# Bias tables fetched a head pair earlier, reciprocals read back in longer pieces, and a planner with dearer transfers through HBM

## The chip, the cores and the metric

The kernel runs on one core of a Trainium2 chip. The core has five engines that work side by side, each through its own list of instructions in order: TensorE (PE in the profile: matrix products into the accumulation banks of PSUM), VectorE (DVE), ScalarE (ACT), GpSimd (POOL) and SyncE (SP). In this kernel SP does nothing but issue transfers (DMA); POOL and, seldom, ACT issue some too. All transfers share the core's 16 DMA engines. An instruction waits until what it reads has been written and until the buffer it writes is free; whatever stands behind it on the same engine waits with it.

The metric is the time of one execution in microseconds (us). Before the change it was measured in three runs, and the median is 567.25 us.

## What is computed

One layer of a hybrid decoder on 512 positions of width 1024, all in fp32: a normalisation, one combined projection, three groups of heads that work in parallel, an output projection, and a feed-forward part.

```python
h = rmsnorm(x, norm1_w)
aq, ak, av, bq, bk, bv, br, ba, cq, ck, cv = split(h @ w_in)
y_a = dilated_attention(aq, ak, av, bias_a)      # 6 heads
y_b = gla(bq, bk, bv, br, ba, ...)               # 4 heads, gated linear attention
y_c = moba_attention(cq, ck, cv, bias_c)         # 6 heads
x = x + concat(y_a, y_b, y_c) @ w_out
x = x + square(relu(rmsnorm(x, norm2_w) @ w_ff1)) @ w_ff2
return rmsnorm(x, final_norm_w)
```

What matters here are the 12 softmax heads of groups A and C. For each head the kernel computes scores q·k, adds a bias that depends only on the distance between query and key (mask and head group are folded into it), takes exp and the row sums, multiplies by v, and divides by the row sums.

## The kernel before, in words

*Precision.* A matrix product of fp32 values is made of three products: each operand is split into a rounded high part and a remainder (`xh`, `xl`, `wh`, `wl`), and high × high, low × high and high × low are added up. So every 512 KB piece of weights is loaded by SP into a `wraw` tile, rounded by ScalarE (`wh`) and subtracted by VectorE (`wl`). This is `parts` (line 310), called by `cut` (332) in a fixed order of pieces.

*Stages.* First the projection for the gated linear attention (up to some 30 us), then the value projection of the first heads, then for each of the six head pairs p = 0 to 5 the query and key projections (`qk_proj`, 1151), the second value projection, the output projection and the feed-forward part, each followed or interleaved by what depends on it. The softmax heads run from some 84 to 206 us, between and beside the projections.

*Attention of a pair.* `attention(e)` (886) runs as two streams, e = 0 and 1, one for each head of a pair. For each pair it takes a buffer `nb` of 128 × 512, and SP loads into it the head's bias table from `tab` in HBM (each partition reads the same row of distances shifted by one, 2 KB). It then waits for the pair's queries and keys, and for four blocks of 128 queries computes scores into one of two score banks (`sps`, tag "s"); `softmax` (983) on VectorE adds the bias from `nb`, takes the minimum and frees the bank, and ScalarE takes exp and the row sum.

*Turning.* The products with the values need the probabilities transposed. For pairs 0 to 3 (`XP`) VectorE transposes blocks of 32 × 32 (`moved`, 1009) into the tiles `tb` and `t2s`, and `through` (1026) puts the blocks in place by way of HBM: SP writes the tile to a scratch `turn`, and POOL reads it back in four transfers into `thb` or `th2` (shown as `th`). Pairs 4 and 5 are transposed on TensorE (`ptp`). `values` (938) multiplies by v for two pairs at a time (`po`).

*Reciprocals.* `row_sums` (990) takes the reciprocals of the row sums, transposes them, and SP writes them to a scratch `zt` in HBM in four transfers of 1 KB. Two reads (`rzb<-zt`) then spread each head's 512 values over 64 partitions. `mix_out` (649) multiplies the value products by them.

*Who sets the order.* The order of instructions on every engine is made when the program is built, by the planner `Plan` (111). The program is a set of Python streams that hand out instructions; the planner keeps a clock for each engine, one for issuing transfers ("dge") and one for the DMA engines as a whole ("dma"), and picks the ready instruction with the earliest start, then by priority. For a transfer, `issue` (140) reckons:

```python
self.clock["dge"] = max(self.clock["dge"], t) + 0.47
self.clock["dma"] = max(self.clock["dma"], self.clock["dge"] + 0.65) + op.size / 360e3
end = self.clock["dma"] + (0.9 if op.eng != "gpsimd" or "accum_op" in op.kw else 4.9)
```

So all bytes move at 360 GB/s one transfer after the other, and data is ready 0.9 us after that, or 4.9 us where POOL issued it. These clocks only make the order; on the chip every instruction waits for its real data.

*Buffers.* `slot` (224) hands out one of 22 buffers of 128 × 512 (`SLOTS`); `nb`, the probabilities, `t2s`, `th2`, `rzb` and many others take theirs from it. The planner does not reckon with waits for a slot; the program adds them. Tiles of 128 × 1024 come from 43 buffers (`big`).

Since the instructions are all issued by the planner, the profile names one line (L141) for nearly all of them, and they are told apart by the names of their tiles.

Of the kernel before, what the change touches and what calls it, by code (L numbers as in the profile page):

```python
# [27 lines left out]
LC, LT, LW, LN, WARM = 1.0, 0.5, 1.0, 0.0, 9  # L28
BIGS, SLOTS, WPAIRS, SCRATCH = 43, 22, 5, 2048
NC = 5  # L30
LATE = ((1, 0),)
XP = (0, 1, 2, 3)
NH = 4
# [74 lines left out]
PE, ACT, DVE, POOL, SP = (Engine(n) for n in ("tensor", "scalar", "vector", "gpsimd", "sync"))  # L108


class Plan:
# [15 lines left out]
    def spawn(self, gen, prio=0):  # L127
        self.streams.append(dict(gen=gen, prio=prio, item=None, at=self.now, sent=None, n=len(self.streams)))

    def fire(self, key, t=None):  # L130
        self.done[key] = self.now if t is None else t

    def give(self, res):
        self.free[res].append(self.now)
# [5 lines left out]
    def issue(self, op, at):  # L140
        getattr(getattr(self.nc, op.eng), op.method)(*op.args, **op.kw)  # L141
        t = self.start(op, at)
        if op.eng in self.part:
            self.part[op.eng] = op.part
        self.clock[op.eng] = end = t + op.cost
        if op.method == "dma_start":
            self.clock["dge"] = max(self.clock["dge"], t) + 0.47
            self.clock["dma"] = max(self.clock["dma"], self.clock["dge"] + 0.65) + op.size / 360e3
            end = self.clock["dma"] + (0.9 if op.eng != "gpsimd" or "accum_op" in op.kw else 4.9)
        for n in op.outs:  # L150
            self.ready[n] = max(self.ready.get(n, 0.0), end + self.LAT)
        return end
# [57 lines left out]
def hybrid_block_kernel(ctx: ExitStack, tc: tile.TileContext, x0_d, xT_d, x_d, w0_d, wv_d, wqk_d, w1_d, w2_d,  # L210
# [13 lines left out]
    def slot(name, dt=F32, shape=(128, 512)):  # L224
        return sp.tile(list(shape), dt, name=name, tag="slot", bufs=SLOTS)

    def big(name, dt=F32, shape=(128, 1024)):
        return wp.tile(list(shape), dt, name=name, tag="big", bufs=BIGS)

    def small(name, shape):  # L230
        return sp.tile(list(shape), F32, name=name, tag="small_" + "_".join(map(str, shape)), bufs=16 if shape[1] <= 2 else 8 if shape[1] == 4 else 3)

    def bank(tag, name):
        return ps.tile([128, 512], F32, name=name, tag=tag, bufs=BANKS[tag])
# [40 lines left out]
    tab = dr.tile([12, 640], F32, name="tab")  # L275
    zr = [[consts.tile([128, 32], F32, name=f"{n}{i}") for n in ("rz", "rzt")] for i in range(2)]
    rzb = {}
# [123 lines left out]
    def fetch2():  # L401
        yield ("wait", ("quad1", 1, (0, 1)))
        for c in range(1, NC):
            last = c == NC - 1
            B[c] = {}
# [37 lines left out]
    def fetch0():  # L443
        yield ("wait", ("qk", 5))
        spawn(sums0(), 3)
        for q in ((0, 0), (1, 1), (0, 1), (1, 0)):
            quads[q] = []
            if q in LATE:
                yield ("wait", "vT")
# [43 lines left out]
    def products(c):  # L493


        if not c:
            return ((0, "X", True, ((0, 0, 1),)), (4, "W", True, ((1, 1, 1),)), (6, "W", False, ((1, 0, 1),)), (2, "X", False, ((1, 0, 1),)),
                    (3, "X", False, ((1, 1, 1),)), (1, "Y", True, ((0, 0, 1),)), (5, "X", False, ((0, 1, 1),)))
        m = ((0, "X", True, ((0, 0, 1),)), (4, "W", True, ((1, 1, -1),)), (1, "Y", True, ((0, 0, 1),)), (6, "W", False, ((1, 0, 1),)),
             (2, "X", False, ((1, 0, 1),)), (3, "X", False, ((1, 1, -1),)), (5, "X", False, ((0, 1, -1),)))  # L500
        return m if c == NC - 1 else m[:3] + m[4:] + m[3:4]

    def cut2(c):
        for o, (n, *_) in enumerate(products(c)):
            if c == NC - 1:
                if o == 0:
# [7 lines left out]
            for _ in range(2):  # L514
                if not c and n not in (0, 4):
                    give("big")
                if c and (n not in (2, 4) and (n != 4) or n == 2 and c == NC - 1):
                    give("big")
# [117 lines left out]
    G = []  # L636
    hs = [{} for _ in range(NC)]

# [247 lines left out]
    def attention(e):  # L886

        yield ("wait", "tab")
        yield ("wait", "attn")
        for p in range(6):  # L890
            nb = slot("nb")
            yield SP.dma_start(nb, bass.AP(tensor=tab.tensor, offset=tab.offset + (2 * p + e) * 640, ap=[[1, 128], [1, 512]]))
            yield ("wait", ("qk", p))
            q2, k2, kl = st[p]
            A0, A1, A2 = slot("P0"), slot("P1"), slot("P2", shape=(128, 256))
            P = [A1[:, 384:512], A2[:, 0:256], A1[:, 0:384], A0[:, 0:512]]
            for qb in (3, 2, 1, 0):
                n = 128 * (qb + 1)
                yield ("take", "s")
                sps = bank("s", "sps")  # L900
                qs = slice(qb * 128, (qb + 1) * 128)
                yield [PE.matmul(sps[:, :n], q2[e][:, qs], k2[e][:, :n], start=True, stop=False),
                       PE.matmul(sps[:, :n], q2[e][:, qs], kl[e][:, :n], start=False, stop=True)]
                if qb == 3:
                    z = small("z", (128, 4))
                    spawn(row_sums(p, e, z), 2)
                spawn(softmax(P[qb], sps[:, :n], nb[:, 384 - 128 * qb:512], (p, e, qb), z), 1)
            if ("sps", p) in plan.done:
                fire(("scored", p))
                give("big")  # L910
                give("big")
                if p == 5:
                    for _ in range(3):
                        give("big")
                    fire("scores")
            fire(("sps", p))
            yield ("take", "big")
            st["th", p, e] = big("thb")
            if p in XP:
                spawn(moved(p, e, P), 1)  # L920
                continue
            for kbs in KBS:
                for qb in range(min(kbs), NB):
                    yield ("wait", (p, e, qb))
                yield ("take", "pt")
                pt = bank("pt", "ptp")
                n = 0
                off = {}
                ops = []
                for kb in kbs:  # L930
                    off[kb] = n
                    for qb in range(kb, NB):
                        ops.append(PE.transpose(pt[:, n:n + 128], P[qb][:, kb * 128:(kb + 1) * 128], flip))
                        n += 128
                yield ops
                spawn(turned(pt, n, off, kbs, (p, e)), 1)
# [46 lines left out]
    def softmax(P, s, nb, key, z):  # L983
        mn = small("mn", (128, 1))
        yield DVE.tensor_tensor_reduce(P, s, nb, 1.0, 3e38, OP.add, OP.min, mn)
        give("s")
        yield ACT.activation(P, P, AF.Exp, bias=mn, scale=-1.0, accum_out=z[:, key[2]:key[2] + 1])
        fire(key)

    def row_sums(p, e, z):  # L990

        for qb in range(NB):
            yield ("wait", (p, e, qb))
        rz, turn = zr[p % 2]
        yield DVE.reciprocal(rz[:, 4 * e:4 * e + 4], z)
        fire(("z", p, e))
        if ("z", p, 1 - e) not in plan.done:
            return
        yield DVE.transpose(turn, rz)
        t = dr.tile([8, 128], F32, name=f"zt{p}")  # L1000
        for a in range(4):
            yield SP.dma_start(t[:, a * 32:a * 32 + 32], turn[a * 32:a * 32 + 8])
        rzb[p] = slot("rzb")
        for e in range(2):
            yield SP.dma_start(rzb[p][64 * e:64 * e + 64].rearrange("r (q c) -> r q c", c=128),
                               bass.AP(tensor=t.tensor, offset=t.offset + 4 * e * 128, ap=[[0, 64], [128, 4], [1, 128]]))
        fire(("rz", p))

    def moved(p, e, P):

        yield ("take", "big")
        t, th = big("tb"), st["th", p, e]
        if ("t2", p) not in st:
            st["t2", p], st["th2", p] = slot("t2s"), slot("th2")
        t2, th2 = st["t2", p], st["th2", p]
        tv, t2v = (x.rearrange("p (k b j) -> p k b j", k=4, j=32) for x in (t, t2))
        for qb, dst in ((3, tv[:, :, :4]), (2, tv[:, :, 4:7]), (1, t2v[:, :, 2 * e:2 * e + 2]), (0, tv[:, :, 7:])):
            yield ("wait", (p, e, qb))
            yield DVE.transpose(dst, P[qb].rearrange("p (b k j) -> p k b j", k=4, j=32))
        yield from through(th, t, 2 * p + e, True)  # L1020
        if ("moved", p) in plan.done:
            yield from through(th2, t2, 12 + p)
            fire(("thx", p))
        fire(("moved", p))
# [755 lines left out]
    spawn(main(), 9)  # L1780
    spawn(gla(), 1)
    spawn(attention(0), 0)
    spawn(attention(1), 0)
    spawn(values(), 0)
    plan.run()
# [82 lines left out]
```

## Time and profile before

| | |
|---|---|
| median of three runs | 567.25 us |
| the three runs | 565.07, 567.25, 569.91 us |
| the profiled execution, its own time | 568.16 us |
| its span, first to last instruction | 566.3 us |
| mean granted clock of TensorE | 0.995 of full speed |
| moved by DMA | 98.82 MB, mean 175 GB/s |

The profile is that of one execution. An engine is busy while it computes; TensorE's matmuls are pipelined, and a busy TensorE can still be slower than it might be where its granted clock is below 1. "SPq" is SP's list of transfers: the time shown is when a transfer was issued and how long the issue took, not when the data landed. A releaser in brackets names what ended the idle time before an instruction. The chain of work that ended last follows the program back from its end, at each step to what released it.

### The profile page before, as it was taken

The page shows a single profiled execution, that of the slowest core. Times are in us where ns is not written, and L with a number is a line of the kernel's source. Part 1 is how long each engine was busy: PE and PEld are TensorE (multiplying, and loading weights), DVE is VectorE, ACT ScalarE, POOL GpSimd, SP SyncE. Part 2 cuts the span into 40 slices and gives each one's busy share as a digit, 9 for nine tenths or more (in the row PEclk, how much of TensorE's full clock was granted, in tenths as well). Part 3 has the DMA queues.
Part 4 walks back from the last instruction along what each step waited for, and adds up shares of the span by engine and source line. Part 5 has one row for each costly group of instructions (what it writes and reads, how often), then busy time and mean ns, then how long its engine had stood idle before and what let it go on. Part 6 is the DMA issues. An engine that isn't in the chain of part 4 may idle for free.

```text
span 566.3 us, 9406 instructions
## 1 busy us (share of the span) xinstructions
PE 551.6 (97%) x3526; PEld 488.1 (86%) x3526; DVE 485.8 (86%) x786; ACT 352.8 (62%) x593; POOL 78.1 (14%) x123
## 2 busy tenths in 40 slices
PE   9999999997997999999999999999999999999995
PEld 8987888886886878899988899988999888999884
DVE  6879999996975799989989958899768999588995
ACT  7646465747583656677885347954468862479654
POOL 7100000161521000200011100111100111102031
PEclk9999999998999999999999999999999999999999
DMA  8940313598788549931559853669814698948504
GB/s 287 396 142 2 112 39 94 164 255 226 243 251 225 191 178 298 311 61 38 185 131 246 191 178 110 164 152 272 238 64 126 163 254 212 220 76 217 116 0 151
DMA packets 32575, 98.82 MB, mean 175 GB/s; under 512 B 4786, under 2 KB 5472, under 8 KB 32528
## 3 DMA queue, kind: packets, MB, share of 16 engines
q1 hardware_dynamic: 24384, 72.45, 37.7%
q0 software_dynamic: 7856, 25.22, 23.3%
q8 instruction: 28, 0.46, 0.3%
q10 hardware_dynamic: 288, 0.53, 0.2%
q14 instruction: 19, 0.16, 0.1%
HBM read 90.80 MB, written 7.40 MB: 173 GB/s over the span
## 4 chain that ended last, share of the span: by engine, by line
PE 89%; DMA 6%; ACT 1%; DVE 1%; issue 1%; SPq 1%; POOL 1%; DVEq 0%; ACTq 0%
PE f2X L141 19%; PE f1V L141 14%; PE f2W L141 10%; PE qkps L141 8%; PE f1W L141 7%; PE vps L141 5%; PE f2Y L141 5%; PE f L141 4%; PE f1X L141 4%; DMA zt<-rzt 3%; PE po L141 2%; PE av L141 2%; DMA wraw<-in_wv 2%; PE sps L141 2%; PE lp L141 1%; PE bk L141 1%
## 5 line engine op out<-in xcount | busy, mean ns | idle before, releaser
L141 POOL DMA_DIRECT2D w2raw<-in_w x36 | 31.7, 905 | 311.1 <-DVE wl L141 188.3
L141 DVE TENSOR_TENSOR wl<-w2raw,wh 128x1024 fp32r<-128x1024 f32 x56 | 68.3, 1236 | 2.6 <-ACT wh L141 2.6
L141 ACT ACTIVATE wh<-w2raw 128x1024 fp32r<-128x1024 f32 x56 | 58.2, 1049 | 18.3 <-PE f2Y L141 12.1
L141 PE MATMUL f2X<-wh,Ah 128*128 128x512 f32 (+1 forms) x160 | 62.3, 389 | 0.0
L141 PE MATMUL f2X<-wh,Al 128*128 128x512 f32 (+1 forms) x160 | 61.9, 387 | 0.0
L141 PE MATMUL f2X<-wl,Ah 128*128 128x512 f32 (+1 forms) x160 | 61.8, 387 | 0.0
L141 ACT ACTIVATE wh<-w1raw 128x1024 fp32r<-128x1024 f32 x42 | 43.3, 1050 | 29.2 <-DVE w1raw L141 27.6
L141 DVE TENSOR_TENSOR wl<-w1raw,wh 128x1024 fp32r<-128x1024 f32 x42 | 50.8, 1220 | 12.4 <-ACT wh L141 12.3
L141 PE MATMUL f1V<-Uh,wh 128*128 128x256 f32 x168 | 47.5, 283 | 0.0
L141 PE MATMUL f1V<-Ul,wh 128*128 128x256 f32 x168 | 47.5, 283 | 0.0
L141 PE MATMUL f1V<-Uh,wl 128*128 128x256 f32 x168 | 47.5, 283 | 0.0
L141 ACT ACTIVATE h<-h 128x512 f32<-128x512 f32 x53 | 33.3, 629 | 17.8 <-DVE h L141 17.1
L141 DVE TENSOR_TENSOR wl<-wraw,wh 128x1024 fp32r<-128x1024 f32 (+1 forms) x32 | 34.5, 1087 | 6.6 <-ACT wh L141 6.5
L141 PE MATMUL qkps<-xh,wh 128*128 128x512 f32 x96 | 38.4, 400 | 0.0
L141 PE MATMUL qkps<-xh,wl 128*128 128x512 f32 x96 | 37.7, 392 | 0.0
L141 PE MATMUL qkps<-xl,wh 128*128 128x512 f32 x96 | 37.6, 392 | 0.0
L141 ACT ACTIVATE P<-P,mn 128x512 f32<-128x512 f32 (+3 forms) x48 | 26.5, 554 | 16.8 <-DVE mn L141 16.7
L141 PEld LDWEIGHTS f2X<-wh,Ah 128*128 128x128 f32 x160 | 30.1, 188 | 6.8 <-issue 1.0
L141 ACT ACTIVATE wh<-wraw 128x1024 fp32r<-128x1024 f32 (+1 forms) x31 | 29.1, 956 | 10.3 <-DMA wraw<-in_wv 10.2
L141 PEld LDWEIGHTS f2X<-wl,Ah 128*128 128x128 f32 x160 | 30.0, 188 | 6.2
L141 PEld LDWEIGHTS f2X<-wh,Al 128*128 128x128 f32 x160 | 30.1, 188 | 5.9
L141 ACT ACTIVATE Ah<-s 128x512 fp32r<-128x512 f32 x40 | 23.8, 623 | 14.3 <-DVE s L141 13.8
(298 smaller groups left out, 1681.2 us busy)
## 6 DMA issues: line engine op xcount, KB each, us to landing
w2raw<-in_w SPq DMA_DIRECT2D x42, 512.0 KB
w2raw<-in_w POOLq DMA_DIRECT2D x36, 512.0 KB, 7.4
w1raw<-in_w SPq DMA_DIRECT2D x28, 512.0 KB
wraw<-in_wqk SPq DMA_DIRECT2D x12, 512.0 KB
wraw<-in_wv SPq DMA_DIRECT2D x8, 512.0 KB
turn<-tb SPq DMA_DIRECT2D x8, 512.0 KB
thb<-turn POOLq DMA_DIRECT2D x32, 128.0 KB, 4.5
woraw<-in_w SPq DMA_DIRECT2D x8, 512.0 KB
```

Of the source, the lines that this page charges most:

```text
L141: getattr(getattr(self.nc, op.eng), op.method)(*op.args, **op.kw)
```

## The change

Three edits. In `attention` each stream now asks for the table of pair p + 1 when it comes to pair p, before it waits for the queries and keys of pair p; at p = 0 it asks for two tables, at p = 5 for none. The number of loads and their size stay the same.

In `row_sums` the read of the reciprocals has as its source one run of 512 elements (2 KB) for each of the 64 partitions, where it had four runs of 128 elements (512 B) that lie one after the other. The same bytes go to the same places.

In `Plan.issue`, a transfer that writes or reads a `turn` scratch counts 1.6 times as long on the clock of the DMA engines; a write to a `zt` scratch counts as landed 6.0 us after its bytes were moved (0.9 before); the 4.9 for transfers issued by POOL gets a name and keeps its value.

```diff
+ZL, PL = 6.0, 4.9
...
-            self.clock["dma"] = max(self.clock["dma"], self.clock["dge"] + 0.65) + op.size / 360e3
-            end = self.clock["dma"] + (0.9 if op.eng != "gpsimd" or "accum_op" in op.kw else 4.9)
+            self.clock["dma"] = max(self.clock["dma"], self.clock["dge"] + 0.65) + op.size / 360e3 * (1 + 0.6 * ("turn" in op.outs[0] + op.ins[0]))
+            end = self.clock["dma"] + (ZL if op.outs[0][:2] == "zt" else 0.9 if op.eng != "gpsimd" or "accum_op" in op.kw else PL)
...
+        nbs = {}
         for p in range(6):
-            nb = slot("nb")
-            yield SP.dma_start(nb, bass.AP(tensor=tab.tensor, offset=tab.offset + (2 * p + e) * 640, ap=[[1, 128], [1, 512]]))
+            for i in range(p, min(p + 2, 6)):
+                if i not in nbs:
+                    nbs[i] = slot("nb")
+                    yield SP.dma_start(nbs[i], bass.AP(tensor=tab.tensor, offset=tab.offset + (2 * i + e) * 640, ap=[[1, 128], [1, 512]]))
+            nb = nbs[p]
             yield ("wait", ("qk", p))
...
         for e in range(2):
-            yield SP.dma_start(rzb[p][64 * e:64 * e + 64].rearrange("r (q c) -> r q c", c=128),
-                               bass.AP(tensor=t.tensor, offset=t.offset + 4 * e * 128, ap=[[0, 64], [128, 4], [1, 128]]))
+            yield SP.dma_start(rzb[p][64 * e:64 * e + 64], bass.AP(tensor=t.tensor, offset=t.offset + 512 * e, ap=[[0, 64], [1, 512]]))
```

## Prediction

> **What bounds the kernel now.** I read in this order: the busy table of the page, the table of busy time by stretches, the timelines of the engines for what ended their idle time, SP's own queue, and last the chain of work that ended last. The busy table:
>
> ```profile
> span 566.3 us, 9406 instructions
> PE 551.6 (97%) x3526; PEld 488.1 (86%) x3526; DVE 485.8 (86%) x786; ACT 352.8 (62%) x593; POOL 78.1 (14%) x123
> ```
>
> TensorE (PE) is busy 97% of the span, and the change gives it no less work, so it can win only idle time and slow clock. Idle are 566.3 − 551.6 = 14.7 us. Four stretches hold nearly all of it (columns: length, busy time and instructions of each engine, granted clock, DMA share, GB/s):
>
> ```profile
> 115.00:130.00 15.00, 14.85 (x68) 12.07 (x66) 12.22 (x25) 5.70 (x10) 7.40 (x14) 1.00 0.99 242
> 130.00:145.00 15.00, 11.86 (x49) 9.68 (x49) 12.04 (x33) 12.11 (x30) 4.21 (x8) 0.89 0.78 234
> 175.00:190.00 15.00, 12.10 (x67) 9.80 (x66) 9.70 (x25) 10.01 (x26) 2.17 (x4) 1.00 0.61 161
> 260.00:566.00 306.00, 299.45 (x1909) 273.44 (x1907) 263.91 (x326) 192.70 (x274) 34.37 (x37) 1.00 0.62 162
> ```
>
> Gap 1, around 130: 0.15 + 3.14 = 3.29 us. Gap 2, after 175: 2.90. The last row: 6.55, the tail of the kernel, where no changed line works. The rest, 2.0, lies elsewhere, mostly at the start. The second row also has a clock of 0.89: 15 × 0.11 = 1.65 us lost. Inside it the clock was halved (third column) for some three us behind the idle time:
>
> ```profile
> 134.00:135.00 1.00, 1.00 (x4) 0.50 1.15 324
> ```
>
> Ceiling of the whole change: 3.29 + 1.65 + 2.90 = **7.84 us**.
>
> **Gap 1, what ends last.** The timeline of ScalarE, VectorE and TensorE, with the idle time before each instruction and its releaser in brackets:
>
> ```profile
> 130.40 1.06 ACT L141 ACTIVATE wh<-wraw 128x1024 fp32r<-128x1024 f32 x1 [7.94 <-DMA wraw<-in_wv]
> ```
> ```profile
> 131.48 1.22 DVE L141 TENSOR_TENSOR wl<-wraw,wh 128x1024 fp32r<-128x1024 f32 x1 [3.64 <-ACT wh L141]
> ```
> ```profile
> 133.11 0.33 PE L141 MATMUL sps<-k,q 128*128 128x128 f32 x1 [3.26 <-DVE mn L141]
> ```
>
> TensorE waits for a score bank. VectorE, whose softmax frees the bank, is held in order behind a weight split, the split behind ScalarE's half of it, and ScalarE stands from 122.46 to 130.40 before a weight piece that SP issued at 119.22, behind two reads of reciprocals:
>
> ```profile
> 117.14 1.65 SPq L141 DMA_DIRECT2D rzb<-zt  x2
> 119.22 0.34 SPq L141 DMA_DIRECT2D wraw<-in_wv  x1
> ```
>
> The piece took 11 us because the DMA engines are full then (share 0.99 at 242 GB/s). The planner reckons 360 GB/s and so put the split ahead of the softmax. A wrong date made the gap, not a lack of work.
>
> **Gap 2.** SP's queue, in order of time:
>
> ```profile
> 161.07 3.35 SPq L141 DMA_DIRECT2D woraw<-in_w  x6
> 164.52 4.05 SPq L141 DMA_DIRECT2D zt<-rzt  x5
> 171.84 0.34 SPq L141 DMA_DIRECT2D nb<-tab  x1
> 173.95 1.87 SPq L141 DMA_DIRECT2D zt<-rzt  x3
> 176.00 0.34 SPq L141 DMA_DIRECT2D turn<-t2s  x1
> 176.39 0.43 SPq L141 DMA_DIRECT2D nb<-tab  x1
> ```
>
> Both bias tables (nb) of the last head pair stand behind six weight loads (3 MB) and five to eight small stores. VectorE's softmax waits for them, and TensorE for the softmax, in two stalls:
>
> ```profile
> 177.38 0.69 DVE L141 CUSTOM_DVE_ANT_0 P<-sps,nb 128x512 f32<-128x512 f32 x1 [0.93 <-DMA nb<-tab]
> ```
> ```profile
> 178.14 0.38 PE L141 MATMUL sps<-k,q 128*128 128x256 f32 x1 [1.81 <-DVE mn L141]
> ```
> ```profile
> 181.97 0.45 PE L141 MATMUL sps<-k,q 128*128 128x384 f32 x1 [1.10 <-DVE mn L141]
> ```
>
> **Part 1, tables one pair ahead.** No load is added or removed: 12 of 256 KB, two for each pair, each issued where the pair before fetched its own. For the load of 171.84 that place is
>
> ```profile
> 139.86 0.37 SPq L141 DMA_DIRECT2D nb<-tab  x1
> ```
>
> 32 us earlier, against 5.5 us from issue to softmax (171.84 to 177.38). So this wait goes: **−2.90**. Late next on VectorE is the subtraction of output weights, which waits for the weight loads; TensorE has projections to do meanwhile. The price is paid at the front, where four loads stand instead of
>
> ```profile
> 85.47 1.75 SPq L141 DMA_DIRECT2D nb<-tab  x2
> ```
>
> 1.75 us more of SP, and whatever SP issues next comes so much later. That next is a weight piece (wraw) right behind; SP's next weight load follows only at 119.22, and TensorE's gaps all lie later, so projections already loaded hide it. I take 0; with that cover gone, 1.75. The tables also hold two of the 22 slots one pair longer, which is rival C.
>
> **Part 2, reciprocals in 2 KB pieces.** 12 reads of 128 KB, the same bytes. The page gives each queue's MB and its share of 16 engines' time; then the packets of 100 to 137 us:
>
> ```profile
> q1 hardware_dynamic: 24384, 72.45, 37.7%
> q0 software_dynamic: 7856, 25.22, 23.3%
> ```
> ```profile
> DMA packets 3316, 8.37 MB, mean 226 GB/s; under 512 B 724, under 2 KB 724, under 8 KB 3312
> ```
>
> SP's queue takes 0.377 × 566.3 / 72.45 = 2.95 us per MB, POOL's 5.23. If 512 B pieces ran at POOL's rate and 2 KB pieces at SP's, a pair of reads (0.26 MB) would save 0.6 us of DMA. The other end is 0: with four of these reads in it, the packet line has none from 512 B to 2 KB, though a packet need not be a piece. I take **0**: the reads lie beside other work everywhere but at 117.14, and there the reordering of part 3 takes the wait away. If it doesn't, 0 to 0.6 us of gap 1 goes. [...]
>
> **Part 3, dearer transfers through HBM.** Nothing runs that did not run, but the order on every queue, SP's and POOL's among them, is made anew. Ahead of the late weight piece SP and POOL had issued since 103 us four turn<-tb, one turn<-t2s of 256 KB and 12 thb:
>
> ```profile
> turn<-tb SPq DMA_DIRECT2D x4, 512.0 KB
> thb<-turn POOLq DMA_DIRECT2D x16, 128.0 KB, 5.4
> ```
>
> Together 2.10 + 0.26 + 1.57 = 3.93 MB, 10.9 us at 360 GB/s and 17.5 with the factor 1.6. The plan now expects the piece 6.6 us later, and ScalarE's wait was 7.94. The 1.3 us left would cost nothing, for ScalarE had stood for 7 us before TensorE ran dry. So softmax and split should change places: −3.29, and with it −1.65, since the stalls of 1.81 and 1.10 us in gap 2 left the clock at 1.00. The bounds are 0 (same order) and 4.94; I take **−4.94**, the error of 7.94 being nearly all in the 6.6.
>
> The read of the reciprocals is planned 5.1 us later (6.0 for 0.9). The store it waits for really took, in the chain,
>
> ```profile
> 113.98 3.07 DMA zt<-rzt
> ```
> ```profile
> 164.87 11.12 DMA zt<-rzt
> ```
>
> so 6.0 lies between, and SP stands less before that read with loads behind it. The scaling of the value products needs it. The last pair is the tightest:
>
> ```profile
> 187.44 1.78 SPq L141 DMA_DIRECT2D zt<-rzt  x4
> ```
> ```profile
> 201.25 0.68 DVE L141 TENSOR_TENSOR h<-po,rzb 128x512 f32<-128x512 f32 x1
> ```
>
> 13.8 us lie between, so 5.1 later is hidden by the value products; without them it costs 5.1.
>
> What is late next: the last turned block of pair 3, from turn<-t2s at 176.00 through POOL's
>
> ```profile
> 178.67 2.17 POOL L141 DMA_DIRECT2D th<-turn  x4 [12.16 <-DVE mn L141]
> ```
> ```profile
> th<-turn POOLq DMA_DIRECT2D x4, 64.0 KB, 5.3
> ```
>
> to the value products
>
> ```profile
> 191.98 4.52 PE po L141 x80
> ```
>
> The last of the four issues is at 180.30 and lands 5.3 later, 185.6: 6.4 us to spare. With TensorE 7.84 us earlier, po is due at 184.1 and waits **1.5 us**. Bounds: 0, if output-projection matmuls are put ahead of it; 4.8, if the block is put behind one more stand of SP such as that from 168.57 to 171.84 (3.3). I take 1.5, what the rows give as they stand.
>
> **Sum.** 566.3 − 4.94 − 2.90 + 0 + 1.5 = 559.96. That execution took 568.16, 1.86 more than its span, and is 0.91 above the median of the three runs, 567.25. So 559.96 + 1.86 − 0.91 = **560.9 us**, 1.1% faster; 559.4 without the new wait, 564.2 with 4.8.
>
> [...]
>
> **Rivals.**
> *A, one gap closes.* For: a list of ready work can still put the split first, as 1.3 us of the wait are not in the factor. Against: gap 2 has a direct cause that part 1 removes. Gap 2 alone: 567.25 − 2.90 = 564.4 (gap 1 alone: 562.3).
> *B, it does not do what it says.* The order keeps gap 1, and new waits eat what the tables save: 567.2.
> *C, slower: early tables hold up SP.* A table takes a slot one pair sooner and keeps it longer. SP has stood for slots already:
>
> ```profile
> SPq L141 <- DVE mn L141: 5.5, 2, 3.5
> ```
>
> up to 3.5 us at once (100 to 112 us), in order, with turned blocks queued behind. It decides at pair 1's block:
>
> ```profile
> 137.31 2.18 POOL L141 DMA_DIRECT2D th<-turn  x4 [10.55 <-ACT P L141]
> ```
> ```profile
> 145.10 4.52 PE po L141 x80
> ```
>
> 138.95 + 5.3 = 144.2, only 0.9 us before its products. From a stand of 0.9 us there on, TensorE waits. Such a stand there and at 191.98 makes stalls like gap 1, 4.94 each: with the old gaps still open, 567.25 + 9.88 = 577.1. Against: that block waited 10.55 us for a slot because ScalarE stood in gap 1, so it comes earlier when gap 1 goes.
>
> **How the numbers follow.** Forecast 0.54, A 0.22, B 0.10, C 0.14. About 1%, 5.7 us, is what a measurement of this kernel can tell from no change: three runs spread from 565.07 to 569.91. The forecast's own range is 559.4 to 564.2; 0.41 of its 0.54 lies below 561.6. Faster 0.41; same 0.13 + 0.22 + 0.10 = 0.45; slower 0.14. The range runs from the ceiling less the 0.9 between runs, 558.5, to B with its runs' scatter, 569.0; C is left out.
>
> **What would show it.** Right: no wait of TensorE over 1 us for VectorE between 125 and 185 us, clock 1.00 throughout; no softmax that waits for nb; pair 2's softmax ahead of the weight split on VectorE; loads of SP between zt and rzb; for part 2, packets as before. Wrong: a new stall ahead of po or the output projection, or SP standing longer than 3.5 us for a slot.

## The result, and the profile after

| | before | after |
|---|---|---|
| median | 567.15 us (14 runs, 565.07 to 570.01) | 562.79 us (14 runs, 560.79 to 565.56) |
| ratio of the times, 95% interval | | 0.9924 [0.9902, 0.9947] |
| the profiled execution: time, span, clock | 568.16 us, 566.3 us, 0.995 | 563.32 us, 561.5 us, 0.995 |

The change makes the kernel 0.8% faster. That is inside the predicted range of 558.5 to 569.0, but 1.9 us above the 560.9 that was forecast. By the prediction's own bound of 1% it would count as no change, to which it gave 0.45; the 14 runs of each tell 0.8% from none all the same. Of the ceiling of 7.84 us the change brought 4.36 (medians) or 4.8 (spans).

One execution with the planner alone (680.44 us, clock 0.753), one with the late date alone (3116.62 us) and two of the kernel before lie far outside their kernels' others and are left out of the medians and ratios below.

The busy table of the changed kernel:

```profile
span 561.5 us, 9386 instructions
PE 551.4 (98%) x3526; PEld 487.5 (87%) x3526; DVE 486.3 (87%) x786; ACT 353.1 (63%) x593; POOL 78.2 (14%) x123
DMA packets 32575, 98.82 MB, mean 176 GB/s; under 512 B 4786, under 2 KB 5472, under 8 KB 32528
```

The work of TensorE is what it was; idle are 561.5 − 551.4 = 10.1 us, against 14.7. The table by stretches shows where (length, busy time and instructions of PE, PEld, DVE, ACT and POOL, clock, DMA share, GB/s):

```profile
115.00:130.00 15.00, 15.00 (x70) 12.61 (x69) 14.79 (x36) 10.62 (x22) 5.48 (x11) 1.00 1.01 286
130.00:145.00 15.00, 15.00 (x76) 12.32 (x76) 14.39 (x46) 13.27 (x35) 6.54 (x12) 1.00 0.95 286
...
160.00:175.00 15.00, 13.31 (x68) 10.82 (x67) 7.93 (x25) 11.21 (x33) 2.17 (x4) 0.89 0.64 238
175.00:190.00 15.00, 15.00 (x110) 12.64 (x111) 11.32 (x13) 6.50 (x11) 0.00 (x0) 1.00 0.65 211
```

Both old gaps are gone: the stretches that held 3.29 and 2.90 us of idle time hold none, and the clock in the second row is 1.00. In their place stands one new stretch, 160 to 175: 1.69 us idle and a clock of 0.89, 15 × 0.11 = 1.65 us. Together 3.34; 7.84 − 3.34 = 4.5, about what was measured.

The timelines of TensorE, VectorE and GpSimd around the new stall:

```profile
168.62 0.33 PE L142 MATMUL sps<-k,q 128*128 128x128 f32 x1 [1.69 <-DVE mn L142]
```
```profile
167.99 0.56 DVE L142 CUSTOM_DVE_ANT_0 P<-sps,nb 128x384 f32<-128x384 f32 x1 [1.62 <-DMA turn<-t2s]
```
```profile
168.43 2.17 POOL L142 DMA_DIRECT2D th<-turn  x4 [11.91 <-DMA turn<-t2s]
```

At first sight the middle row makes no sense: a softmax of the last pair reads `sps` and `nb`, neither of which has to do with the turning of pair 3. What it waits for is room. It writes a `P` buffer, and by this row that buffer is the slot in which pair 3's `t2s` still lies (the experiments with more slots, below, bear it out); `t2s` is free only when the store that reads it is done. SP's queue and the chain of waits (start, length, what) show how long that took:

```profile
156.23 3.02 SPq L142 DMA_DIRECT2D woraw<-in_w  x6
159.30 0.43 SPq L142 DMA_DIRECT2D turn<-t2s  x1
```
```profile
159.30 8.56 DMA turn<-t2s
...
167.99 0.56 DVE P L142
...
168.62 0.44 PE sps L142 x2
```

The store of 256 KB was issued behind six weight loads (3 MB), and 8.56 us lie between its issue and its end. A planner that does not reckon with slots can't see this wait.

Behind the stall the clock was 0.50 for some three us. Windows of one microsecond of TensorE alone (length, busy time and instructions, clock, DMA share, GB/s):

```profile
168.00:169.00 1.00, 0.39 (x3) 1.00 0.27 97
...
170.00:171.00 1.00, 1.00 (x6) 0.50 0.55 143
171.00:172.00 1.00, 1.00 (x3) 0.50 0.28 86
172.00:173.00 1.00, 1.00 (x4) 0.50 0.00 0
```

By the mean clock that didn't happen in each run. Six of the 14 had a mean clock of 0.997 or 0.998 and took 560.79 to 561.81 us, 561.5 on the mean; eight had 0.994 or 0.995 and took 562.75 to 565.56, 564.0 on the mean. Only the profiled run, one of the eight, shows where the clock was lost.

### The profile page after: what moved, and what is told of

The parts are those of the page before. It is cut to its first block, busy times and chain, and to the rows that moved or that the text cites. A ratio compares the mean times of both kernels' runs of the same rounds, so it can differ in the third digit from the quotient of the medians.

```text
span 561.5 us, 9386 instructions
## 1 busy us (share of the span) xinstructions
PE 551.4 (98%) x3526; PEld 487.5 (87%) x3526; DVE 486.3 (87%) x786; ACT 353.1 (63%) x593; POOL 78.2 (14%) x123
## 2 busy tenths in 40 slices
DMA packets 32575, 98.82 MB, mean 176 GB/s; under 512 B 4786, under 2 KB 5472, under 8 KB 32528
## 4 chain that ended last, share of the span: by engine, by line
PE 96%; DMA 2%; DVE 1%; issue 0%; ACT 0%; DVEq 0%; SPq 0%; ACTq 0%
PE f2X L142 19%; PE f1V L142 14%; PE qkps L142 12%; PE f2W L142 10%; PE vps L142 8%; PE f1W L142 7%; PE f2Y L142 5%; PE f L142 4%; PE f1X L142 4%; PE po L142 2%; PE sps L142 2%; PE av L142 2%; DMA turn<-t2s 2%; PE lp L142 1%; PE bk L142 1%; PE bq L142 1%
## 5 line engine op out<-in xcount | busy, mean ns | idle before, releaser
L142 PEld LDWEIGHTS f1V<-Uh,wh 128*128 128x128 f32 x168 | 32.3, 192 | 0.0
```

## The experiments

All ratios are to the kernel before, with their 95% intervals. The questions: which part took which gap away, what made the new stall, and whether a version without any stall can be had.

### Each part alone

**Tables alone** (the kernel before with the edit of `attention` from the change, nothing else).

> Part 1 alone, on the kernel before. Theory (late tables make gap 2, a wrong date makes gap 1): no softmax waits for nb any more, gap 2 (2.9 us) goes; the planner's dates are the old ones, so VectorE still stands behind the weight split and gap 1 with its slow clock stays: 567.2 - 2.9 = 564.3 us. Rival (early tables hold slots, so what they save comes back as waits for a slot): 567 us or more, with a wait of VectorE or SP for a slot that is longer than before.

564.65 us (12 runs), 0.996 [0.9938, 0.9983]. Both gaps went, not only gap 2: though the planner's dates are the old ones, SP's queue came out in another order, with the reads of reciprocals (122.96) behind the late weight piece (118.69). A new stall took back some three quarters of what the gaps had cost: 4.11 us idle and 1.80 lost to the clock, of 7.84. The timelines of TensorE and ScalarE and the chain of waits:

```profile
172.24 1.45 PE L141 MATMUL ptp<-cst,P 128*128 128x128 f32 x8 [4.11 <-ACT th L141]
```
```profile
171.81 0.38 ACT L141 ACTIVATE th<-ptp 128x256 f32<-128x256 f32 x1 [4.87 <-DMA turn<-t2s]
```
```profile
159.47 12.25 DMA turn<-t2s
```

It is the stall of the changed kernel in a longer form. ScalarE wants a slot for a transposed block, `t2s` of pair 3 still occupies it, and its store takes 12.25 us behind the six weight loads. So the new stall belongs to the early tables, which hold two slots longer.

**Pieces alone** (the kernel before with the edit of `row_sums`; the order of the instructions is that of before).

> Part 2 alone, on the kernel before; the order of every queue is that of before. Theory (packets were whole rows already): packet counts as before (5472 under 2 KB), 567.2 us, within 0.3%. Rival (512 B pieces are slow): reads of the reciprocals take less DMA time, gap 1 shrinks by up to 0.6 us, 566.6 us.

566.63 us (12 runs), 0.9991 [0.9974, 1.0009]: no difference. Both gaps stay, and but for one packet the page counts what it counts for the kernel before and for the changed kernel (32575):

```profile
DMA packets 32574, 98.82 MB, mean 175 GB/s; under 512 B 4786, under 2 KB 5472, under 8 KB 32528
```

**Planner alone** (the kernel before with the edits of `Plan.issue`).

> Part 3 alone: dearer transfers on the planner's clocks, tables and pieces as before. Theory: gap 1 and its slow clock go (4.9 us), gap 2 stays since the last tables still stand behind six weight loads: 562.3 us and a softmax that waits for nb around 175 us. Rival (the new order alone does all of it): 562.8 us or less, and no softmax waits for nb.

563.46 us (10 runs), 0.9931 [0.9911, 0.9952]. The rows below are from one further execution of the same kernel.

> Part 3 alone once more, for a profile at full clock. Theory: no gap 1; the softmax of the last pair waits for nb behind the weight loads, TensorE idle 1 to 3 us around 170 to 180. Rival: no wait for nb, and a wait for a slot in its place.

565.15 us in that one run. It turns the prediction's attribution round: gap 2 is gone, though the first table of the last pair is issued as late as before (171.69, before 171.84; the second at 174.01, before 176.39), and gap 1 is still there in another form. The timelines of TensorE, VectorE and ScalarE:

```profile
134.87 0.44 PE L142 MATMUL sps<-k,q 128*128 128x384 f32 x1 [2.48 <-DVE mn L142]
```
```profile
133.99 0.45 DVE L142 STREAM_TRANSPOSE t2s<-P 128x256 f32<-128x256 f32 x1 [2.53 <-ACT wh L142]
```
```profile
126.61 1.06 ACT L142 ACTIVATE wh<-wraw 128x1024 fp32r<-128x1024 f32 x1 [4.13 <-DMA wraw<-in_wv]
```

ScalarE waits 4.13 us for the weight piece instead of 7.94, and runs late by that much. VectorE is held no longer by the weight split but by a transposition that waits for ScalarE, and TensorE again waits for a score bank. The profile names ScalarE's next rounding (132.87) as what released the transposition; that it was really the exp just ahead of it (132.38), whose result is transposed, is likely and not shown.

### What made the new stall: slots

**The change with more slots.** 24 slots of 128 × 512; one buffer of 128 × 1024 less pays for the two. The order on TensorE and SP is that of the changed kernel.

```diff
-BIGS, SLOTS, WPAIRS, SCRATCH = 43, 22, 5, 2048
+BIGS, SLOTS, WPAIRS, SCRATCH = 42, 24, 5, 2048
```

> The changed kernel with 24 slots and 42 large buffers for 22 and 43. TensorE's and SP's orders stay the same, and those of the other engines up to the feed-forward part. Theory (the new stall of TensorE at 168.6 is a wait for a slot: VectorE's softmax of the last pair writes where t2s still is being read by a transfer queued behind six weight loads): no such wait with two more slots, stall (1.69) and slow clock behind it (1.65) gone, span about 558.2, median about 560.2, and mean clock 0.997 or more in every run. Rival (the transfer itself is late, whatever the slot): another wait takes its place, 562 us or more.

560.64 us (6 runs, 559.85 to 561.73), 0.9888 [0.9865, 0.9912]. The stall is gone, and with it the slow clock (all six runs 0.997 or 0.998). Its row for the stretch of the stall:

```profile
160.00:175.00 15.00, 15.00 (x89) 12.50 (x89) 9.75 (x30) 13.65 (x38) 2.18 (x4) 1.00 0.67 251
```

**Tables alone with 24 slots** (the same line changed in the kernel with the tables alone).

> Part 1 alone with 24 slots and 42 large buffers; TensorE's and SP's orders are those of part 1 alone. Theory (the stall of 4.1 us that part 1 alone has is the same wait for t2s's slot): stall and slow clock gone, 560.5 us as the changed kernel with more slots, so part 3 is worth nothing once slots are there. Rival (the new order has a share of its own): 562 us or more.

560.64 us (6 runs), 0.9893 [0.986, 0.9925], no stall. Where slots suffice, the tables alone do all that the whole change does, and the pieces and the planner's new costs add nothing.

**24 slots alone** (the same line changed in the kernel before).

> The kernel before with 24 buffers of 128 x 512 in place of 22 (and 42 of 128 x 1024 in place of 43), nothing of the change; the order on TensorE and SP stays that of before. Theory (the two gaps come from what stands in SP's queue ahead of a weight piece and of the last tables, and slots matter only once the order is mended): gap 1 stays, at some 130 us with 3 us and the clock halved behind it; gap 2 stays or loses at most the 1 to 2 us in which SP stands before the table of 171.84; 565.5 to 567.2, ratio 0.997 to 1.000. Rival 1 (SP stands for slots, and that makes both gaps): both go, 560.6 as with the change and 24 slots, ratio 0.989. Rival 2 (gap 2 alone is made by slots): 564.3, ratio 0.995.

567.35 us (12 runs), 1.0018 [0.9996, 1.004]. Slots by themselves are worth nothing: the gaps of before were not waits for a slot. They stay, with 2.60, 1.65 and 1.54 us of idle time before three score products.

**The store of t2s earlier.** The changed kernel hands out POOL's read-backs of the pair's last `tb` between the store of that `tb` and the store of `t2s`; here SP writes `t2s` right behind `tb` (the core of the edit; `...` marks what is left out):

```diff
-        yield from through(th, t, 2 * p + e, True)
-        if ("moved", p) in plan.done:
-            yield from through(th2, t2, 12 + p)
...
+        d = dr.tile([128, t.shape[1]], F32, name=f"turn{2 * p + e}")
+        yield SP.dma_start(d, t)
...
+        if both:
+            d2 = dr.tile([128, t2.shape[1]], F32, name=f"turn{12 + p}")
+            yield SP.dma_start(d2, t2)
+        yield from through(th, d)
```

> The changed kernel with the store of t2s issued right behind that of tb, before POOL's read-backs are planned, so that for pair 3 it stands ahead of the six weight loads in SP's queue. Theory (the stall at 168.6 waits for a slot that this store holds, 8.6 us long because weights are ahead of it): the store lands in about 5 us, VectorE does not wait for it, stall 1.69 and slow clock 1.65 gone: about 560.2 us, clock 0.997 or more. Rival (late turned blocks or slots make another wait): 562 us or more.

562.11 us (6 runs, 560.84 to 565.05), 0.9916 [0.9884, 0.9949]. In the profiled run the stall near 168 us and the slow clock were gone and two short ones (0.54 and 0.32 us) had come earlier; span 559.1. But the median is only 0.7 us below the changed kernel's, within the scatter of both. The order moved in other places too, so this stays inconclusive as to the time.

### What took gap 1 away: the two halves of part 3

**The late date of the reciprocals' store alone.**

```diff
-            end = self.clock["dma"] + (0.9 if op.eng != "gpsimd" or "accum_op" in op.kw else 4.9)
+            end = self.clock["dma"] + (6.0 if op.outs[0][:2] == "zt" else 0.9 if op.eng != "gpsimd" or "accum_op" in op.kw else 4.9)
```

> The kernel before with one number of part 3 alone: the store of the reciprocals counts as landed 6.0 us after its bytes, not 0.9 (no factor 1.6, tables and pieces as before). Theory (gap 1 comes from SP standing before the reads of the reciprocals with weight pieces behind them): the reads move behind the weight pieces, the late piece lands by about 126 us, gap 1 and its slow clock go, gap 2 stays: 562.3 us. Rival (the factor 1.6 corrects the date): gap 1 stays, about 567 us.

564.12 us (11 runs), 0.9957 [0.9929, 0.9984]. Gap 1 is gone but for 0.46 us. SP's queue shows why:

```profile
116.90 0.44 SPq L141 DMA_DIRECT2D wraw<-in_wv  x1
...
121.78 2.51 SPq L141 DMA_DIRECT2D rzb<-zt  x2
```

The two reads of reciprocals, which stood ahead of the late weight piece (117.14 before 119.22), now stand behind it, and ScalarE rounds that piece at 123.90 without a wait. Gap 2 stays, still for the tables:

```profile
180.39 0.69 DVE L141 CUSTOM_DVE_ANT_0 P<-sps,nb 128x512 f32<-128x512 f32 x1 [2.64 <-DMA nb<-tab]
```

**The factor 1.6 alone.**

```diff
-            self.clock["dma"] = max(self.clock["dma"], self.clock["dge"] + 0.65) + op.size / 360e3
+            self.clock["dma"] = max(self.clock["dma"], self.clock["dge"] + 0.65) + op.size / 360e3 * (1 + 0.6 * ("turn" in op.outs[0] + op.ins[0]))
```

> The kernel before with the factor 1.6 on transfers through turn alone: no late store of reciprocals, old tables, old pieces. The step of the prediction was that this factor sets the date of the late weight piece 6.6 us later and so puts softmax ahead of the split. By that step gap 1 and its slow clock go (4.94) and gap 2 stays: 562.3, ratio 0.991. Rival (what stands ahead of the weight piece in SP's queue decides, and the factor does not move the reads of reciprocals): a wait of ScalarE of over 4 us for a weight piece and a stall of TensorE of over 2 us stay between 125 and 140 us; 565 to 567.5, ratio 0.996 to 1.000.

560.46 us (6 runs, 560.30 to 561.80), 0.9895 [0.9873, 0.9917]: by the medians this one line alone beats the whole change by 2.3 us (the two intervals just overlap), and both theories on record were off, for both gaps went. The stretches of old gaps 1 and 2, and SP's queue and ScalarE at the old gap 1:

```profile
130.00:145.00 15.00, 15.00 (x76) 12.39 (x74) 13.99 (x44) 11.93 (x29) 4.37 (x8) 1.00 0.82 260
...
175.00:190.00 15.00, 14.99 (x140) 12.96 (x139) 11.97 (x28) 9.65 (x25) 0.00 (x0) 1.00 0.44 122
```
```profile
116.78 0.36 SPq L141 DMA_DIRECT2D wraw<-in_wv  x1
117.65 1.85 SPq L141 DMA_DIRECT2D zt<-rzt  x4
119.61 0.83 SPq L141 DMA_DIRECT2D wraw<-in_wv  x2
121.36 3.47 SPq L141 DMA_DIRECT2D rzb<-zt  x2
```
```profile
124.45 1.06 ACT L141 ACTIVATE wh<-wraw 128x1024 fp32r<-128x1024 f32 x1 [2.62 <-DMA wraw<-in_wv]
```

The reads stand behind three weight pieces, and ScalarE's wait falls from 7.94 to 2.62. VectorE's timeline shows that softmax and split did not change places: the split still comes first, but in time.

```profile
126.47 0.56 DVE L141 CUSTOM_DVE_ANT_0 P<-sps,nb 128x384 f32<-128x384 f32 x1 [0.39 <-PE sps L141]
...
127.03 1.22 DVE L141 TENSOR_TENSOR wl<-wraw,wh 128x1024 fp32r<-128x1024 f32 x1
128.17 0.42 DVE L141 CUSTOM_DVE_ANT_0 P<-sps,nb 128x256 f32<-128x256 f32 x1
```

As for gap 2, both tables of the last pair are issued earlier than before (at 171.84 and 176.39 there), though still behind the six weight loads, which start at 154.54. VectorE does work on output weights first, and the first softmax of each head of the pair runs without a wait, at 174.81 and 177.38. SP's queue and VectorE:

```profile
162.42 0.33 SPq L141 DMA_DIRECT2D nb<-tab  x1
...
172.02 0.34 SPq L141 DMA_DIRECT2D nb<-tab  x1
```
```profile
172.54 2.35 DVE L141 TENSOR_TENSOR woraw<-woraw 128x1024 f32<-128x1024 f32 x2
174.81 0.68 DVE L141 CUSTOM_DVE_ANT_0 P<-sps,nb 128x512 f32<-128x512 f32 x1
...
177.38 0.68 DVE L141 CUSTOM_DVE_ANT_0 P<-sps,nb 128x512 f32<-128x512 f32 x1
```

### The parts taken from the whole

**The change with the old pieces** (without the edit of `row_sums`; its order is that of the changed kernel).

> The changed kernel with the reciprocals read in the old 512 B pieces; the order of all instructions is that of the changed kernel. Theory (the pieces are worth nothing in either order): 562.8, ratio to before 0.992, the stall of about 1.7 us for turn<-t2s near 168 us as in the changed kernel. Rival (longer pieces free DMA time where the engines are full): up to 0.6 us for a pair of reads where one is on the path, 563.4 to 564.0, ratio 0.993 to 0.995, and rows of rzb<-zt that take longer to land.

561.63 us (6 runs), 0.9917 [0.9892, 0.9942]: the pieces are worth nothing in this order either. The same softmax waits for the same store, but more briefly, and TensorE with it:

```profile
167.90 0.33 PE L142 MATMUL sps<-k,q 128*128 128x128 f32 x1 [1.04 <-DVE mn L142]
```

Here the clock stayed at 1.00, and 561.04 us in the profiled run is like the faster six runs of the changed kernel.

**The change without the late date.**

```diff
-ZL, PL = 6.0, 4.9
+ZL, PL = 0.9, 4.9
```

> The changed kernel without the late date of the reciprocals' store (0.9 again in place of 6.0); early tables, 2 KB pieces and the factor 1.6 stay. The factor alone reached 560.5, the whole change 562.8. Theory (the tables, which hold two buffers one pair longer, cost the 2.3: they leave the last pair's softmax or its turned blocks waiting for a buffer that the late store of t2s still reads): the kernel stays above 561.5, with a stall of TensorE of 1 us or more behind DMA turn<-t2s between 160 and 180 us; 562 to 564.6, ratio 0.991 to 0.996. Rival (the late date costs them, by moving the store of t2s behind more of SP's queue): no such stall, 560.5, ratio 0.989.

568.19 us (12 runs), 1.0022 [1.0001, 1.0043]. The theory had the direction and not the size: beside the factor alone (560.46, in another series), the tables and the pieces cost some 7 to 8 us, and the pieces are worth nothing in the two orders where they were tried alone. There are two stalls, each with a clock of 0.50 behind it (137 to 140 us and 175 to 177). VectorE at the first, TensorE at both:

```profile
134.55 0.69 DVE L142 CUSTOM_DVE_ANT_0 P<-sps,nb 128x512 f32<-128x512 f32 x1 [2.75 <-DMA turn<-t2s]
```
```profile
135.31 0.39 PE L142 MATMUL sps<-k,q 128*128 128x256 f32 x1 [2.00 <-DVE mn L142]
```
```profile
174.33 0.58 PE L142 MATMUL sps<-k,q 128*128 128x256 f32 x1 [3.02 <-DVE mn L142]
```

The first is again a slot held by a store of `t2s`. For the second the profile names no releaser of VectorE; that it is the store of 166.88, whose read-back by POOL starts at 174.03, is argued and not shown.

### All of it in one table

For each profiled run: the idle time of TensorE and the time lost to the clock, worked out from its seven rows of 15 us between 100 and 205 us (15 less the busy time; 15 times what the clock lacks of 1.00), and what is left of the span.

| kernel | median, us | span | idle | clock | rest |
|---|---|---|---|---|---|
| before | 567.15 | 566.3 | 6.19 | 1.65 | 558.5 |
| 24 slots alone | 567.35 | 565.8 | 6.03 | 1.65 | 558.1 |
| pieces alone | 566.63 | 566.2 | 6.48 | 1.65 | 558.1 |
| change without the late date | 568.19 | 566.5 | 5.10 | 3.45 | 558.0 |
| late date alone | 564.12 | 565.9 | 4.10 | 1.65 | 560.2 |
| tables alone | 564.65 | 564.2 | 4.11 | 1.80 | 558.3 |
| factor and late date | 563.46 | 563.4 | 2.48 | 1.65 | 559.3 |
| **the change** | 562.79 | 561.5 | 1.69 | 1.65 | 558.2 |
| change, t2s stored first | 562.11 | 559.1 | 0.86 | 0 | 558.2 |
| change with old pieces | 561.63 | 559.2 | 1.04 | 0 | 558.2 |
| change with 24 slots | 560.64 | 559.2 | 0 | 0 | 559.2 |
| tables with 24 slots | 560.64 | 558.7 | 0 | 0 | 558.7 |
| factor alone | 560.46 | 558.6 | 0.01 | 0 | 558.6 |

(Factor and late date is the planner alone; its median is that of the ten runs, the rest that of the one further execution. The medians come from several series, in which the kernel before had 566.49 to 567.15.) But for one kernel, at 560.2, the rest lies between 558.0 and 559.3, and that one lost 1.7 us to the clock elsewhere: its stretch from 42 to 56 us has a clock of 0.88. So nothing of the change speeds up any work. Each order has its own stalls in the attention stage, and the time is some 558.5 us and these stalls. The parts don't add up: the tables win 2.5 us in the order of before and lose some 7 to 8 in that of the factor (with the pieces); the late date costs 3.0 us beside the factor and wins 5.4 where the tables and the pieces are there too.

## Why the prediction was right, and where it was not

*The ceiling* of 7.84 us was right, and so was the reading that TensorE can win only idle time and slow clock: the three kernels without a stall have spans 7.1 to 7.7 us below that of before.

*Part 1, −2.90.* Right in that no softmax waits for `nb` any more and in that the front costs nothing that shows: the four loads take SP 2.33 us where two took 1.75, and TensorE has no idle time from 85 to 100 us. That the tables are what took gap 2 away in the changed kernel is only half shown, since the factor without them takes it away as well. The price was elsewhere. That the tables "hold two of the 22 slots one pair longer" was noted, but only as rival C, with SP standing for slots ahead of pair 1's block. What waited was VectorE, in the last pair, for a slot that a store still read.

*Part 2, 0.* Right, in both orders: 0.9991 [0.9974, 1.0009] in that of before, and 561.63 us with the old pieces against 562.79 with the new in that of the change. The packet counts are the same with either length of piece (5472 under 2 KB on each page), so what packets of 512 B cost beside longer ones was not shown.

*Part 3, −4.94.* The end was right in the changed kernel (gap 1 gone, clock 1.00 there), and the mechanism was wrong. "So softmax and split should change places" did not come about. The split moved the other way, ahead of the 384-wide softmax that had run before it (127.20 and 131.48 in the kernel before), and it came in time:

```profile
126.88 1.22 DVE L142 TENSOR_TENSOR wl<-wraw,wh 128x1024 fp32r<-128x1024 f32 x1
128.01 0.55 DVE L142 CUSTOM_DVE_ANT_0 P<-sps,nb 128x384 f32<-128x384 f32 x1
```

What changed was SP's queue, named in the prediction only as something to look for ("loads of SP between zt and rzb"). In the three orders with the reads of reciprocals ahead of the late piece (before, pieces alone, 24 slots alone), 10.5 to 11.4 us lie between the issue of the piece and its rounding by ScalarE. In the seven with the reads behind it where ScalarE still waits for the piece, it is 6.0 to 9.0 us. An earlier issue isn't needed for that: the change with 24 slots and the change without the late date issue the piece at 119.26 and 119.74, no earlier than before (119.22), and ScalarE waits 2.45 and 2.69 us; the pieces alone issue it at 118.54, still behind the reads, and ScalarE waits 7.03. Nor was it that "the DMA engines are full then": in the changed kernel their share in that stretch is 1.01, against 0.99. Whether the reads themselves held the piece up, or other transfers that moved with them, no run takes apart. Nor did the prediction see that the factor by itself removes gap 2 as well.

*The new wait, +1.5.* The transfer was named rightly, the `turn<-t2s` of pair 3. The wait was not: the sum has TensorE's value products wait for the turned block, reckoned with a store at 176.00. In the changed kernel that store was issued at 159.30 and POOL's read-back by 170.6, and the products ran at 187.26 without a wait. What waited was the softmax that took over the store's slot, a wait for a buffer that no term of the sum holds. That it came to 1.69 us, so near 1.5, is luck.

*The term that was mis-sized* is the same one. It was put at 1.5 us with no slow clock behind it; the prediction had noted that stalls of 1.81 and 1.10 us left the clock at 1.00. Behind the stall of 1.69 us it was 0.50 in the profiled run, so the term is 1.69 + 1.65 = 3.34. By spans, 559.96 + 1.84 = 561.8, and 561.5 was measured. The median, 562.79, lies at the lower edge of the eight runs with the lower mean clock; the six with the higher one took 561.5 on the mean, 0.6 from the forecast.

*The signs.* Those that held: no softmax waits for `nb`, loads of SP stand between `zt` and `rzb`, packets are as before. Those that failed: TensorE waits 1.69 us for VectorE, the clock falls to 0.89 in one stretch, and the softmax isn't ahead of the split.

## What to carry to other kernels

A planner that reckons with data but not with buffers can turn an earlier fetch into a wait for a buffer somewhere else: when a load is moved forward, look up which buffers stay taken longer, who takes the next one, and which slow store still reads it. When an edit changes a hand-made or planned order, measure its parts alone and with one taken away, for they don't add up: here one line of a three-part change, or one part with two more buffers, gave 6.5 to 6.7 us where the whole gave 4.4. Price a stall of TensorE with the slow clock that may follow it: here 1.65 us behind one of 1.69 in the profiled run.

## What the hardware showed that was not expected

*Short stalls and the clock.* A stall of 1.69 us was followed by a clock of 0.50 in the changed kernel, one of 2.00 us by the same in the change without the late date. One of 2.93 us in the kernel with the pieces alone was not: its stretch keeps 1.00. First a window behind the stall of 2.00, then the stretch with the one of 2.93:

```profile
137.00:138.00 1.00, 1.00 (x4) 0.50 0.96 381
```
```profile
175.00:190.00 15.00, 10.92 (x62) 1.00 0.61 158
```

The columns are length, busy time of TensorE, clock, DMA share and GB/s. So the length of a stall, between 1.7 and 3 us, did not decide here; what does was not tried.

In the profiled run of the late date alone the clock was also 0.50 at 51 us, where the kernel before has 1.00. TensorE's waits for a score bank all come after 136 us in that run, and none of its three others is over 1.1 us:

```profile
51.00:52.00 1.00, 1.00 (x4) 0.50 0.00 0
```

*Stores behind loads.* A store of 256 KB took 8.56 and 12.25 us from issue to end where six weight loads (3 MB) had been issued just ahead of it on the same queue. In both rows the instruction that needed the source buffer started only after that.
